# Token tiles loaded from ScalarE's queue beside weights from SyncE's, and two reordered places in a one-core hybrid block

## The chip, the cores and the metric

The kernel runs on one core of a Trainium2 chip. The metric is the device time of one execution in microseconds (us), lower is better. Five engines share the core's on-chip memory: TensorE (PE, matmuls into PSUM), VectorE (DVE), ScalarE (ACT), GpSimd (POOL) and SyncE (SP, which here does little but issue transfers). Each engine works through its own list of instructions in order; semaphores make one wait for another. A DMA is issued by an engine and then carried out by 16 DMA engines beside it.

## What is computed

One layer of a hybrid encoder block on 256 tokens of width 2048, float32. Cut to what matters:

```
u = rms_norm(x, norm_mix_pre)
proj = u @ w_in                        # q/k/v of two attentions, RWKV-7 inputs, three gates
y_a = stick_breaking_attention(...);  y_b = forgetting_attention(...);  y_c = rwkv7_time_mix(...)
m = g_a * (y_a @ w_branch_a) + g_b * (y_b @ w_branch_b) + g_c * (y_c @ w_branch_c)
x = x + rms_norm(m @ w_out, norm_mix_post)
hdn = square(relu(rms_norm(x, norm_mlp_pre) @ w_mlp_up))        # 2048 -> 8192
x = x + rms_norm(hdn @ w_mlp_down, norm_mlp_post)
```

The change touches the first lines (how `x` and the first weights come in), the step from `m @ w_out` to `w_mlp_up`, and the last line.

## The kernel before, in words

**Weights.** All weights lie in one array `wst` of pieces of 128 x 1024 floats (512 KB). They stream through three buffers `raw`. Each piece is split into a rounded high part (`whi`, an ACT copy) and the rest (`wlo`, a DVE subtraction); activations are split the same way into the two halves of a tile `pk`. A product is then high x both halves (a matmul of 512 columns) and low x high (256 columns). `wsplit` (L151) does the split; a new piece may be loaded only when the DVE has read the old one out of its buffer.

**Who decides the order.** A scheduler places the instructions on the engines; in the first part, up to `written.close()` (L1273), PE's order is the order in which the code is written. `tc.issue_after` makes an instruction come after a named one on its engine. A DMA gets one of eight completion semaphores in turn, and an issue whose semaphore still belongs to an earlier DMA waits until that one has landed, on the queue of the engine that issues it.

**Begin** (L264 to L369). The token matrix, transposed, is `X0`: 16 tiles of 128 x 256 (tile k holds features 128k to 128k+127). `loadx(a, b)` loads tiles a to b-1, `load(n, q)` half q of weight piece n, `con` and `ident` are constants. All of these are issued by SP. Three products `qb` are built at once: pieces 0, 2, 4 with tiles 0 to 7, then pieces 1, 3, 5 with tiles 8 to 15. `xsplit(k)` (L311) makes `pk` of tile k, `wpart` (L319) splits half a piece, `prods` (L328) issues the matmuls. Five matmuls on zeros (L273) run before the data come.

**Passage** (L1166 to L1272). For the second half of the tokens (`tt` = 1) the residual sum `x1[1]` is finished in strips of 256 columns (`add_mixed`, L1182, DVE) while it is already transposed and used. In the loop over k2 = 0, 2, ... 14, `turned(k2, 1)` (L1220) transposes two 128 x 128 blocks of `x1[1]` into one half of the PSUM tile `trs[k2 // 2]`; ACT and DVE read that tile into two tiles `pk` (L1254, L1260); and `both(k2 - 2)` (L1230) runs the eight matmuls of the two tiles before with two weight pieces. The blocks of the first token half are transposed by `turn_first` (L1223), which also takes a new PSUM tile. There are four such tiles (`mps`, four buffers): four `turn_first` come before the loop, and the fifth, sixth, ... need a tile that ACT and DVE have read to the end.

**End** (L1592 to L1619). The last product comes in two token halves of 128 rows. For each half, for the last strip of 512 columns: DVE adds PSUM into `y` (L1603), ACT squares with a running sum (L1604), `rstd_of` turns that into a factor `rs` (DVE L1165, POOL L1166), `gained` multiplies by the gain (L1607), and four DVE instructions of 512 columns (L1618) each followed by a store of 256 KB (L1619) give the output.

Of the kernel before, what the change touches and what calls it, by code (L numbers as in the profile page):

```python
# [12 lines left out]
AF = mybir.ActivationFunctionType  # L13
ALU = mybir.AluOpType
# [4 lines left out]
D = 2048  # L19
# [31 lines left out]
def hybrid_block(ctx, tc, xt, x, gains, params, consts, lora, gup, wst, out):  # L51
    nc = tc.nc
    V, A, G, PE = nc.vector, nc.scalar, nc.gpsimd, nc.tensor
# [11 lines left out]
    def nm(s):  # L65
        uid[0] += 1
        return f"{s}_{uid[0]}"
# [15 lines left out]
    par = cpool.tile([128, NPAR], F32, name="par")  # L83
# [7 lines left out]
    def P(name, i=0, r=slice(0, 128)):  # L91
        return par[r, PC[name] + i:PC[name] + i + 1]
# [135 lines left out]
    def pin(ins):  # L228
        return tc.keep_in_program_order(ins)
# [33 lines left out]

    dum = cpool.tile([128, 1], F32, name="dum")  # L264
    G.memset(dum, 0.0)
    A.activation(dum, dum, AF.Tanh)
    X0 = rp.tile([128, KT, T], F32, tag="SC", name="x0", bufs=1)
    A6 = rp.tile([128, 6, T], F32, tag="b6", name="a6", bufs=1)
    zt = rp.tile([128, T], F32, tag="tha", name="zt", bufs=1)
    V.memset(zt, 0.0)  # L270
    idle = mps()
    for i in range(5):
        PE.matmul(idle[:, 0:T], zt[:, 0:128], zt, start=True, stop=True)  # L273
    nc.sync.dma_start(out=par, in_=params)
    raws = {}

    def load(n, q=None):

        if n not in raws:
            raws[n] = wpool.tile([128, HALF], F32, tag="raw", name=nm("raw"), bufs=3)  # L280
        cs = slice(0, HALF) if q is None else slice(512 * q, 512 * q + 512)
        nc.sync.dma_start(out=raws[n][:, cs], in_=wst[n][:, cs])

    def loadx(a, b):
        nc.sync.dma_start(out=X0[:, a:b, :], in_=xt[:, a:b, :])

    loadx(0, 2)
    load(0, 0)
    loadx(2, 4)
    load(2, 0)  # L290
    load(4, 0)
    loadx(4, 8)
    for n in (0, 2, 4):
        load(n, 1)
    loadx(8, 12)
    side.append(lambda: nc.sync.dma_start(out=con, in_=consts[:, 128:]))
    side.append(lambda: nc.sync.dma_start(out=ident, in_=consts[:, 0:128]))
    cst = cpool.tile([128, 4], F32, name="cst")
# [12 lines left out]
    def xsplit(k):  # L311
        u = pk()
        split(X0[:, k, :], u, P("g1", k))
        upk.append(u)

    qb = [gps() for _ in range(3)]
    w = {}
# [92 lines left out]
    for h in range(8):  # L410
        ps = qb[h] if h < 3 else unit(upk)
# [641 lines left out]
    for s in ("q", "k"):  # L1053
        lst = []
        for h in range(4):
            ps = unit(upk)
# [12 lines left out]
    for hf in range(2):  # L1069
        for s, mo in (("k", MU_K), ("r", MU_R), ("v", MU_V)):  # L1070
            for p in range(4 * hf, 4 * hf + 4):
                ps = unit(upk)
# [84 lines left out]
    def rstd_of(ss, eps, sums):  # L1157

        if sums is None:
            sums = cpool.tile([128, 1], F32, name=nm("ssum"))  # L1160
            V.tensor_reduce(sums, ss[:, 0:3], AX.X, ALU.add)
            V.tensor_scalar(sums, sums, 1.0 / D, eps, ALU.mult, ALU.add)
            return sums
        r = cpool.tile([128, 1], F32, name=nm("rs"))
        V.tensor_scalar(r, ss[:, 3:4], 1.0 / D, sums, ALU.mult, ALU.add)  # L1165
        G.tensor_tensor(r, r, cst[:, 2:3], ALU.pow)  # L1166
        return r

    g2, loads = gain(0, [fm().rearrange("p a b -> p (a b)")[:, 0:512] for _ in range(4)])
    x1 = [p2.tile([128, D], F32, tag="x1", name=nm("x1"), bufs=2) for _ in range(2)]  # L1170
    for c in range(0, D, 512):
        for tt in range(2):
            loads.append(lambda tt=tt, c=c: nc.sync.dma_start(out=x1[tt][:, c:c + 512],
                                                              in_=x[tt * 128:tt * 128 + 128, c:c + 512]))
# [15 lines left out]
    for g in range(4):  # L1190
# [4 lines left out]
        for tt, ps in enumerate(tok(mpk, 5 if g == 3 else 1)):  # L1195
            def gained():
                return V.tensor_tensor(mg[tt][:, gs], ps, g2[g], ALU.mult)
# [18 lines left out]
    trs = []  # L1216
# [6 lines left out]
    def turn_first():  # L1223
        trs.append(mps())
        turned(2 * len(trs) - 2, 0)
# [23 lines left out]
    for k2 in range(0, KT, 2):  # L1249
        turned(k2, 1)  # L1250
        src = [trs[k2 // 2][:, i * T:i * T + T] for i in range(2)]
        us = [pk(), pk()]
        for i, u in enumerate(us):
            queued(0, lambda: A.activation(u[:, 0:T], src[i], AF.Copy, scale=P("g3", k2 + i)))  # L1254
        if k2 == 8:
            queued(1, pend)
        if k2 + 2 < KT:
            queued(1, lambda: add_mixed(1, 128 * k2 + 256, 256))
        for i, u in enumerate(us):
            queued(1, lambda: V.scalar_tensor_tensor(u[:, T:], src[i], P("g3", k2 + i), u[:, 0:T].bitcast(F32),  # L1260
                                                     ALU.mult, ALU.subtract))
        upk2.extend(us)
        if k2:
            both(k2 - 2)
        if len(trs) < 8:
            turn_first()
        if k2 in (2, 6, 10):
            with tc.issue_after(chain[0].ins), tc.issue_after(chain[1].ins):
                wsplit(wraw(base + {2: 1, 6: 3, 10: 4}[k2]))
            if k2 < 10:  # L1270
                whl.append(wq.pop(0))
# [65 lines left out]
    eps4, sum4 = [], []  # L1337
    ss4 = cpool.tile([128, 2, 4], F32, name="ss4")
    ys = []
# [177 lines left out]
    for j in range(2):  # L1517
        up(j)
        ps, post = heads[j]
# [72 lines left out]
    for g in range(4):  # L1592
        gs = slice(512 * g, 512 * g + 512)
        if g == 2:
            assert not threads
            spare.clear()
            x1 = [p2.tile([128, D], F32, tag="x1", name=nm("x1"), bufs=2) for _ in range(2)]
            for tt in range(2):
                for c in (0, 1024):
                    nc.sync.dma_start(out=x1[tt][:, c:c + 1024], in_=xs[tt][:, c:c + 1024])  # L1600
        for tt, ps in enumerate(tok(hp, 3 if g == 3 else 1)):
            yv = ys[tt][:, gs]
            V.tensor_tensor(yv, yv, ps, ALU.add)  # L1603
            A.activation(junk(), yv, AF.Square, accum_out=ss4[:, tt, g:g + 1])  # L1604

            def gained():
                V.tensor_tensor(yv, yv, g4[g], ALU.mult)  # L1607

            if g < 3:
                gained()  # L1610
                if g == 2:
                    sum4.append(rstd_of(ss4[:, tt, :], eps4[tt], None))
            else:
                r4 = rstd_of(ss4[:, tt, :], None, sum4[tt])
                gained()
                for c in range(0, D, 512):
                    cs = slice(c, c + 512)
                    V.scalar_tensor_tensor(x1[tt][:, cs], ys[tt][:, cs], r4, x1[tt][:, cs], ALU.mult, ALU.add)  # L1618
                    nc.sync.dma_start(out=out[tt * 128:tt * 128 + 128, cs], in_=x1[tt][:, cs])  # L1619


# [123 lines left out]
```

## Time and profile before

| What | Value |
|---|---|
| Time, three runs | 1502.9, 1503.46 (median), 1503.58 us |
| Profiled execution | 1500.87 us, span 1499.1 us |
| Mean granted TensorE clock | 0.997 |
| Busy: DVE | 1215.9 us (81%) |
| Busy: ACT | 934.6 us (62%) |
| HBM read / written | 282.65 MB / 4.19 MB |

The span runs from the first to the last instruction of the profiled execution; the execution's own time is 1.77 us longer. In the views below, times are us from the start of the span. A row of the timeline gives start, length, engine, line, operation, the tile written and those read, how many instructions were merged, and in brackets how long the engine had been idle before it and what ended that. "SPq" is SP issuing a DMA.

### The profile page before, as it was taken

Reading aid. Unit: us, or ns where it says so; the run is one execution under the profiler, and the core shown is the slowest. Engines: PE = TensorE matmul, PEld = TensorE weight load, DVE = VectorE, ACT = ScalarE, POOL = GpSimd, SP = SyncE. Lnnn points to the kernel's source line nnn. Section 1 sums busy time; section 2 is a strip of 40 time slices with the busy share of each in tenths; the row PEclk is TensorE's granted clock in tenths of the full one; section 3 lists DMA queues with packets and bytes.
Section 4 is the critical chain, followed back from the end, with each engine's and each line's share of the span. In section 5 each row is a group of like instructions: output and inputs, shape, how many; then the busy total and the mean of one; then the engine's idle time right before and its main releaser. Section 6 shows DMA issues by size and latency. Waiting matters only on the chain.

```text
span 1499.1 us, 22798 instructions
## 1 busy us (share of the span) xinstructions
PE 1479.3 (99%) x8401; PEld 1248.4 (83%) x8401; DVE 1215.9 (81%) x1687; ACT 934.6 (62%) x1396; POOL 91.2 (6%) x160
## 2 busy tenths in 40 slices
PE   9999999999999999999998999999999999999997
PEld 7888888888778888788887888888888888888885
DVE  7576678899679798567646788999899989899986
ACT  7565666664576554474444766777767766767662
POOL 0021000100001100000000000000000000000000
PEclk9999999999999999999999999999999999999999
DMA  7545545445544546445755868888888888889874
GB/s 267 191 152 188 170 169 183 168 162 195 172 156 168 177 166 209 143 159 189 275 191 181 278 216 250 253 253 264 240 257 246 269 252 233 254 241 266 279 244 152
DMA packets 107615, 317.70 MB, mean 212 GB/s; under 512 B 10736, under 2 KB 14704, under 8 KB 107248
## 3 DMA queue, kind: packets, MB, share of 16 engines
q1 hardware_dynamic: 94832, 284.91, 55.1%
q0 software_dynamic: 8064, 29.36, 10.5%
q10 hardware_dynamic: 4608, 1.97, 0.5%
q8 instruction: 66, 1.08, 0.3%
q14 instruction: 45, 0.37, 0.1%
HBM read 282.65 MB, written 4.19 MB: 191 GB/s over the span
## 4 chain that ended last, share of the span: by engine, by line
PE 94%; DVE 2%; DMA 1%; ACT 1%; issue 1%; POOL 0%; SPq 0%; POOLq 0%; DVEq 0%; ACTq 0%
PE gps L220 28%; PE gps L174 22%; PE gps L178 12%; PE gps L204 7%; PE mps L1469 3%; PE mps L1470 3%; PE mps L1471 3%; PE gps L1471 2%; PE gps L1469 2%; PE gps L1470 2%; PE gps L182 1%; DMA x<-in_xt_dram 1%; DMA raw<-in_wst_dram 1%; PE mps L789 1%; DVE wlo L159 1%
## 5 line engine op out<-in xcount | busy, mean ns | idle before, releaser
L159 DVE TENSOR_TENSOR wlo<-raw,whi 128x1024 fp32r<-128x1024 f32 x497 | 602.7, 1221 | 152.1 <-ACT whi L158 136.8
L158 ACT ACTIVATE whi<-raw 128x1024 fp32r<-128x1024 f32 x497 | 523.0, 1057 | 247.9 <-PE gps L220 85.4
L174 PE MATMUL gps<-pk,whi 128*128 128x512 f32 x1336 | 336.5, 391 | 0.4 <-ACT whi L158 0.4
L174 PEld LDWEIGHTS gps<-pk,whi 128*128 128x128 f32 x1336 | 247.3, 188 | 48.8 <-ACT whi L158 0.6
L220 PE MATMUL gps<-whi,pk 128*128 128x512 f32 x1136 | 286.0, 391 | 0.0
L220 PEld LDWEIGHTS gps<-whi,pk 128*128 128x128 f32 x1136 | 211.5, 188 | 44.0
L178 PEld LDWEIGHTS gps<-pk,wlo 128*128 128x128 f32 x1424 | 194.1, 190 | 14.1 <-DVE wlo L159 0.3
L178 PE MATMUL gps<-pk,wlo 128*128 128x256 f32 x1424 | 199.3, 282 | 0.0
L220 PE MATMUL gps<-wlo,pk 128*128 128x512 f32 x568 | 155.2, 392 | 0.0
L220 PEld LDWEIGHTS gps<-wlo,pk 128*128 128x128 f32 x568 | 105.6, 188 | 21.9
L1332 DVE TENSOR_TENSOR sp<-raw,sp 128x1024 fp32r<-128x1024 f32 x67 | 81.8, 1220 | 3.3 <-ACT sp L1331 3.1
L1360 ACT ACTIVATE sp<-gps 128x512 f32<-128x512 f32 x52 | 31.0, 597 | 83.0 <-PE gps L182 83.0
L1331 ACT ACTIVATE sp<-raw 128x1024 fp32r<-128x1024 f32 x67 | 70.7, 1055 | 14.3 <-PE mps L1470 4.7
L204 PE MATMUL gps<-whi,pk 128*128 128x512 f32 x256 | 68.9, 390 | 0.0
L1469 PE MATMUL mps<-whi,fm 128*128 128x512 f32 x168 | 66.1, 394 | 0.0
L1470 PE MATMUL mps<-whi,fm 128*128 128x512 f32 x168 | 65.8, 392 | 0.0
L1471 PE MATMUL mps<-wlo,fm 128*128 128x512 f32 x168 | 65.5, 390 | 0.0
L1431 POOL DMA_DIRECT2D raw<-raw x40 | 34.9, 874 | 431.6 <-DVE wlo L159 106.7
L204 PEld LDWEIGHTS gps<-whi,pk 128*128 128x128 f32 x256 | 47.8, 188 | 9.9
L1471 PE MATMUL gps<-wlo,fm 128*128 128x512 f32 x126 | 49.3, 391 | 0.4 <-DVE wlo L159 0.4
L1469 PE MATMUL gps<-whi,fm 128*128 128x512 f32 x126 | 49.2, 391 | 0.0
L1428 DVE TENSOR_TENSOR raw<-raw,raw 128x1024 f32<-128x1024 f32 x40 | 48.8, 1221 | 0.4
(390 smaller groups left out, 2006.0 us busy)
## 6 DMA issues: line engine op xcount, KB each, us to landing
raw<-in_wst_dram SPq DMA_DIRECT2D x499, 512.0 KB, 4.3
raw<-raw POOLq DMA_DIRECT2D x40, 512.0 KB, 6.6
sp<-in_wst_dram SPq DMA_DIRECT2D x16, 512.0 KB, 5.5
raw<-sp POOLq DMA_DIRECT2D x8, 512.0 KB, 6.7
sp<-raw POOLq DMA_DIRECT2D x8, 512.0 KB, 6.9
x<-in_x_dram SPq DMA_DIRECT2D x8, 256.0 KB, 5.5
xs<-x SPq DMA_DIRECT2D x2, 1024.0 KB, 4.3
x<-xs SPq DMA_DIRECT2D x4, 512.0 KB, 5.9
```

Of the source, the lines that this page charges most:

```text
L158: A.activation(hi, raw, AF.Copy)
L159: V.tensor_tensor(lo, raw, hi.bitcast(F32), ALU.subtract)
L174: PE.matmul(ps, hi[:, i * 128:i * 128 + 128], pks[i], start=first and i == 0, stop=False)
L178: PE.matmul(ps[:, 0:T], lo[:, i * 128:i * 128 + 128], pks[i][:, 0:T], start=False, stop=False)
L204: PE.matmul(ps[tt], pks[k][:, c:c + 128], w[:, (k - k0) * 512:(k - k0) * 512 + 512], start=k == 0 and part == 0 and w is hl[0], stop=w is ...
L220: PE.matmul(ps[tt], pks[k][:, c:c + 128], w[:, (k - k0) * 512:(k - k0) * 512 + 512], start=k == 0 and part == 0 and w is hl[0], stop=False)
L1331: A.activation(hi, raw, AF.Copy)
L1332: V.tensor_tensor(lo, raw, hi.bitcast(F32), ALU.subtract)
L1428: V.tensor_tensor(x, x, z, ALU.add)
L1469: PE.matmul(Q[f], p, w, start=d == 0 and i == 0, stop=False)
L1470: PE.matmul(Q[f], pl, w, start=False, stop=False)
L1471: PE.matmul(Q[f], p, wl, start=False, stop=d == nd - 1 and i == 1)
```

## The change

Three edits.

1. Begin: the loads of token tiles 0 to 11 move from SP's queue to ACT's: two loads of two tiles each, then the small activation `warm` (which loads ACT's function table), then two loads of four tiles each. SP issues the parameters, the six weight halves, and then what follows; tiles 12 to 15 stay on SP.
2. Passage: `turn_first` inside the loop is moved under `if k2:`, so that it is not called at k2 = 0.
3. End: of the four last DVE instructions of token half 0, two stay where they were and two come after the DVE addition of half 1 (`added`). For half 1 the last strip of 512 columns is done as two of 256.

```diff
-    A.activation(dum, dum, AF.Tanh)
     X0 = rp.tile([128, KT, T], F32, tag="SC", name="x0", bufs=1)
+    def loadx(a, b, queue=nc.sync):
+        return queue.dma_start(out=X0[:, a:b, :], in_=xt[:, a:b, :])
+    nc.sync.dma_start(out=par, in_=params)
+    for a in (0, 2):
+        first_x = loadx(a, a + 2, nc.scalar)
+    with tc.issue_after(first_x.ins):
+        warm = A.activation(dum, dum, AF.Tanh)
+    with tc.issue_after(warm.ins):
+        for a in (4, 8):
+            last_x = loadx(a, a + 4, nc.scalar)
...
-    loadx(0, 2)
-    load(0, 0)
-    loadx(2, 4)
-    load(2, 0)
-    load(4, 0)
-    loadx(4, 8)
-    for n in (0, 2, 4):
-        load(n, 1)
-    loadx(8, 12)
+    for q in range(2):
+        for n in (0, 2, 4):
+            load(n, q)
...
         if k2:
             both(k2 - 2)
-        if len(trs) < 8:
-            turn_first()
+            if len(trs) < 8:
+                turn_first()
...
-            V.tensor_tensor(yv, yv, ps, ALU.add)
+            added = V.tensor_tensor(yv, yv, ps, ALU.add)
...
-            else:
-                r4 = rstd_of(ss4[:, tt, :], None, sum4[tt])
+                continue
+            def final(c, w):
+                cs = slice(c, c + w)
+                V.scalar_tensor_tensor(x1[tt][:, cs], ys[tt][:, cs], r4, x1[tt][:, cs], ALU.mult, ALU.add)
+                nc.sync.dma_start(out=out[tt * 128:tt * 128 + 128, cs], in_=x1[tt][:, cs])
+            if tt == 0:
+                r4 = rstd_of(ss4[:, 0, :], None, sum4[0])
                 gained()
-                for c in range(0, D, 512):
+                final(0, 512)
+                final(512, 512)
+                r40 = r4
+                continue
+            with tc.issue_after(added.ins):
+                for c in (1024, 1536):
                     cs = slice(c, c + 512)
-                    V.scalar_tensor_tensor(x1[tt][:, cs], ys[tt][:, cs], r4, x1[tt][:, cs], ALU.mult, ALU.add)
-                    nc.sync.dma_start(out=out[tt * 128:tt * 128 + 128, cs], in_=x1[tt][:, cs])
+                    V.scalar_tensor_tensor(x1[0][:, cs], ys[0][:, cs], r40, x1[0][:, cs], ALU.mult, ALU.add)
+                    nc.sync.dma_start(out=out[0:128, cs], in_=x1[0][:, cs])
+            r4 = rstd_of(ss4[:, 1, :], None, sum4[1])
+            gained()
+            for c, w in ((0, 512), (512, 512), (1024, 512), (1536, 256), (1792, 256)):
+                final(c, w)
```

The change adds lines, so a line number of the kernel after is up to 17 higher than that of the same statement before.

SP's list at the begin from the last weight half on, before (`x` is the token matrix X0, `raw` a weight piece or its half):

```order
L282 DMA raw_103<-in_wst_dram 128x512
L285 DMA x_86<-in_xt_dram 128x1024
L282 DMA raw_213<-in_wst_dram 128x1024
L285 DMA x_86<-in_xt_dram 128x1024
L282 DMA raw_216<-in_wst_dram 128x1024
L282 DMA raw_218<-in_wst_dram 128x1024
L145 DMA raw_312<-in_wst_dram 128x1024
```

and now:

```order
L292 DMA raw_105<-in_wst_dram 128x512
L269 DMA x_85<-in_xt_dram 128x1024
L297 DMA con<-in_consts_dram 128x1152
L298 DMA ident<-in_consts_dram 128x128
L292 DMA raw_213<-in_wst_dram 128x1024
L292 DMA raw_216<-in_wst_dram 128x1024
L292 DMA raw_218<-in_wst_dram 128x1024
L145 DMA raw_312<-in_wst_dram 128x1024
```

Four token loads are gone from SP. Tiles 12 to 15 stood behind `raw_213` (piece 1) and now stand ahead of it, and so do the two constants, which the scheduler had placed behind pieces 6 and 7.

ACT's list at the begin now (before, it began with the table load):

```order
L269 DMA x_85<-in_xt_dram 128x512 x2
L275 ACT_TABLE_LOAD
L275 ACTIVATE dum<-dum 128x1
L269 DMA x_85<-in_xt_dram 128x1024 x2
L242 ACTIVATE pk_123<-x_85,par 128x256
```

All four issues stand ahead of ACT's first work; the last of them has the semaphore of the first weight half and waits until that has landed.

PE's list in the passage, before (`x_1337` and `x_1338` are the two token halves of `x1`, `mps` are the tiles `trs`):

```order
L1220 MATMUL mps_7982<-ident,x_1338_7310 128x128 x2
L1220 MATMUL mps_8004<-ident,x_1337_7309 128x128 x2
L1220 MATMUL mps_7985<-ident,x_1338_7310 128x128 x2
L1235 MATMUL gps_7980<-pk_7997,whi_7918 128x512
L1235 MATMUL gps_7981<-pk_7997,w_1464_7940 128x512
L1235 MATMUL gps_7980<-pk_7998,whi_7918 128x512
L1235 MATMUL gps_7981<-pk_7998,w_1464_7940 128x512
L1239 MATMUL gps_7980<-pk_7997,wlo_7919 128x256
L1239 MATMUL gps_7981<-pk_7997,w_1465_7941 128x256
L1239 MATMUL gps_7980<-pk_7998,wlo_7919 128x256
L1239 MATMUL gps_7981<-pk_7998,w_1465_7941 128x256
L1220 MATMUL mps_8024<-ident,x_1337_7309 128x128 x2
```

and now:

```order
L1221 MATMUL mps_7982<-ident,x_1338_7310 128x128 x2
L1221 MATMUL mps_7985<-ident,x_1338_7310 128x128 x2
L1236 MATMUL gps_7980<-pk_7997,whi_7918 128x512
L1236 MATMUL gps_7981<-pk_7997,w_1464_7940 128x512
L1236 MATMUL gps_7980<-pk_7998,whi_7918 128x512
L1236 MATMUL gps_7981<-pk_7998,w_1464_7940 128x512
L1240 MATMUL gps_7980<-pk_7997,wlo_7919 128x256
L1240 MATMUL gps_7981<-pk_7997,w_1465_7941 128x256
L1240 MATMUL gps_7980<-pk_7998,wlo_7919 128x256
L1240 MATMUL gps_7981<-pk_7998,w_1465_7941 128x256
L1221 MATMUL mps_8021<-ident,x_1337_7309 128x128 x2
L1221 MATMUL mps_7988<-ident,x_1338_7310 128x128 x2
```

The first row of each is `turned(0, 1)`. The fifth `turn_first` (`mps_8004`, now `mps_8021`) has moved behind the first `both` (the eight rows of L1235 and L1239, now L1236 and L1240), and every later one moves back by one `both` as well. On DVE one pair changes places in the passage: the weight subtraction of k2 = 2 now stands ahead of the strip of `add_mixed` that it followed.

DVE's list at the end, before (`rs` are the factors of the two halves):

```order
L1618 SCALAR_TENSOR_TENSOR x_2583_14109<-y_8767,rs_14256,x_2583_14109 128x512 x4
L1603 TENSOR_TENSOR y_8768<-y_8768,gps_14204 128x512
L1165 TENSOR_SCALAR rs_14289<-ss_8164,ssum_14200 128x1
L1607 TENSOR_TENSOR y_8768<-y_8768,pk_13934 128x512
L1618 SCALAR_TENSOR_TENSOR x_2584_14110<-y_8768,rs_14289,x_2584_14110 128x512 x4
```

and now:

```order
L1618 SCALAR_TENSOR_TENSOR x_2583_14109<-y_8767,rs_14256,x_2583_14109 128x512 x2
L1604 TENSOR_TENSOR y_8768<-y_8768,gps_14204 128x512
L1631 SCALAR_TENSOR_TENSOR x_2583_14109<-y_8767,rs_14256,x_2583_14109 128x512 x2
L1166 TENSOR_SCALAR rs_14289<-ss_8164,ssum_14200 128x1
L1608 TENSOR_TENSOR y_8768<-y_8768,pk_13934 128x512
L1618 SCALAR_TENSOR_TENSOR x_2584_14110<-y_8768,rs_14289,x_2584_14110 128x512 x3
L1618 SCALAR_TENSOR_TENSOR x_2584_14110<-y_8768,rs_14289,x_2584_14110 128x256 x2
```

The addition of half 1 stands two instructions earlier, the factor of half 1 where it stood, and there is one final instruction and one store more.

More of the change, by code (lines that the diff above doesn't have):

```diff
@@ L273, in hybrid_block @@
         PE.matmul(idle[:, 0:T], zt[:, 0:128], zt, start=True, stop=True)
-    nc.sync.dma_start(out=par, in_=params)
     raws = {}
@@ L282, in load @@
         nc.sync.dma_start(out=raws[n][:, cs], in_=wst[n][:, cs])
-    def loadx(a, b):
-        nc.sync.dma_start(out=X0[:, a:b, :], in_=xt[:, a:b, :])
-    loadx(0, 2)
-    load(0, 0)
-    loadx(2, 4)
-    load(2, 0)
-    load(4, 0)
-    loadx(4, 8)
-    for n in (0, 2, 4):
-        load(n, 1)
-    loadx(8, 12)
+    for q in range(2):
+        for n in (0, 2, 4):
+            load(n, q)
     side.append(lambda: nc.sync.dma_start(out=con, in_=consts[:, 128:]))
```

## The prediction

> **What bounds the kernel now.** The page's chain of work that ended last comes first, then the view of waits for PE:
>
> ```profile
> PE 94%; DVE 2%; DMA 1%; ACT 1%; issue 1%; POOL 0%; SPq 0%; POOLq 0%; DVEq 0%; ACTq 0%
> ```
>
> ```profile
> PE mps L1220 <- DVE pk L1260: 3.0, 3, 1.9
> PE gps L334 <- DVE pk L243: 1.5, 2, 1.3
> ```
>
> The whole program is one long stretch of PE work. PE's named waits are few, and the longest ones lie in just the places that the change edits: L334 is the begin, L1220 the passage. Elsewhere PE always has work, so what is won or lost at these places moves everything behind it by as much. The third place is the tail after PE's last matmul, where DVE, POOL and the stores follow each other. So I price three stages apart and add.
>
> **Begin.** The timeline, then the chain in order of time, the windows, and two transfers, each from a stretch that holds its issue alone (KB, us to landing):
>
> ```profile
> 4.21 0.91 ACT L242 ACTIVATE pk<-x,par 128x256 fp32r<-128x256 f32 x2 [1.98 <-DMA x<-in_xt_dram]
> 5.02 0.61 ACT L325 ACTIVATE whi<-raw 128x512 fp32r<-128x512 f32 x1
> 7.13 0.91 ACT L242 ACTIVATE pk<-x,par 128x256 fp32r<-128x256 f32 x2 [1.49 <-DMA x<-in_xt_dram]
> 12.07 0.33 SPq L282 DMA_DIRECT2D raw<-in_wst_dram  x1
> 13.07 1.70 ACT L242 ACTIVATE pk<-x,par 128x256 fp32r<-128x256 f32 x4
> 17.86 1.70 PE L334 MATMUL gps<-pk,whi 128*128 128x512 f32 x4 [0.25 <-DVE pk L243]
> ```
>
> ```profile
> 19.55 0.96 PE gps L332 x8
> 20.51 1.84 PE gps L334 x8
> ```
>
> ```profile
> 0.00:7.00 7.00, 5.73 (x12) 3.70 (x12) 2.28 (x7) 2.91 (x5) 2.18 (x15) 1.00 0.59 183
> 7.00:12.00 5.00, 3.79 (x21) 3.18 (x22) 3.74 (x8) 4.26 (x9) 0.00 (x0) 1.00 0.96 375
> 12.00:13.00 1.00, 1.00 (x8) 0.71 (x7) 1.00 (x4) 1.00 (x3) 0.00 (x0) 1.00 0.12 49
> ```
>
> ```profile
> raw<-in_wst_dram SPq DMA_DIRECT2D x1, 512.0 KB, 3.2
> x<-in_xt_dram SPq DMA_DIRECT2D x1, 512.0 KB, 6.8
> ```
>
> The last three numbers of a windows row are the granted clock, the busy share of the DMA engines and GB/s. Until 12 us ACT waits for data again and again; then SP has nothing to issue, because the next buffer is free only at 12.07, and the DMA engines stand nearly idle for 1 us. Piece 1 lands 3.2 us after its issue, at 15.27, and tiles 12 to 15, issued behind it, hold PE: its first matmuls on them at 17.86 run at DVE's pace, 1.70 us for four where eight take 1.84. From there PE runs through, and the group of piece 1 ends at 19.55 + 0.96 = 20.51.
>
> Now tiles 12 to 15 come before piece 1, so PE's group of piece 1 hangs on piece 1 alone. If that lands at L, ACT copies half of it (0.61), and PE needs 1.84 + 0.96: the group ends at L + 3.4. It breaks even at L = 17.1; the begin is worth 17.1 - L.
>
> L by bytes: ahead of piece 1 now stand the parameters (58 KB), all of x (2048), six halves of 256, `con` (576) and `ident` (64), with piece 1 itself 4794 KB, or 4.91 MB. By 12 us the trace had moved 7 x 183 + 5 x 375 = 3156, or 3.16 MB. The other 1.75 MB at 375 GB/s take 4.7 us, to 16.7. A landing comes later than the bytes' turn: piece 1, with little ahead of it, took 3.2 where its 512 KB at 375 GB/s take 1.4, and of the 1.8 between I count 0.8 as behind the last byte. Since two engines issue side by side, data start about one issue earlier, 0.4 (0.33 in the row of 12.07, and a gap). That is **L = 17.1, begin 0.0 us**. So what x's last tiles gain, the constants ahead of piece 1 use up; PE did not need them that early.
>
> Bounds: piece 1 is of no use before ACT has made the seven tiles that stand ahead of it, from 13.07 at 1.70 / 4 each, 16.0, which gives +1.1. At worst piece 1 takes as long as the slowest load here, 6.8 from 12.07: L = 18.9, -1.8. The four issues on ACT cost it some 0.4 us each ahead of its first copy, and the last waits for the first weight half (there by the copy of 5.02 before), so the first copy moves from 4.21 to 5.3 or more. This is covered: ACT waits for tiles 2 and 3 till 7.13 anyway. If that cover went, at most the 1.49 us of that row would be lost. The five matmuls on zeros, the table load and the parameters do not move on the path.
>
> The Trainium skill, "DMA: Bandwidth & Descriptors", section Issuing engines are not separate DMA queues, says that queues of several engines run on the same 16 DMA engines and that a second one saves only issue time; it speaks against this edit. By that rule the begin is worth no more than the 0.0 above, and a rate better than 183 GB/s in the first 7 us is not to be had.
>
> **Passage.** Timeline, chain and windows:
>
> ```profile
> 810.33 0.44 PE L1220 MATMUL mps<-ident,x 128*128 128x128 f32 x2 [1.30 <-DVE x L1182]
> 810.81 0.84 ACT L1254 ACTIVATE pk<-mps,par 128x256 fp32r<-128x256 f32 x2 [1.92 <-PE mps L1220]
> 811.68 0.88 DVE L1260 SCALAR_TENSOR_TENSOR pk<-mps,par,pk 128x256 fp32r<-128x256 f32 x2 [1.01 <-ACT pk L1254]
> 812.47 0.48 DVE L1182 SCALAR_TENSOR_TENSOR x<-mg,rs,x 128x256 f32<-128x256 f32 x1
> 812.70 1.01 PE L1220 MATMUL mps<-ident,x 128*128 128x128 f32 x4 [1.93 <-DVE pk L1260]
> 821.01 0.68 DVE L1197 TENSOR_TENSOR mg<-gps,fm 128x512 f32<-128x512 f32 x1
> 821.61 1.22 DVE L159 TENSOR_TENSOR w<-raw,w 128x1024 fp32r<-128x1024 f32 x1
> ```
>
> ```profile
> 813.71 1.71 PE gps L1235 x4
> 815.42 0.85 PE gps L1239 x4
> ...
> 825.57 0.93 PE gps L1235 x4
> 826.50 0.47 PE gps L1239 x4
> 826.96 0.22 PE mps L1220 x2
> 827.18 1.83 PE gps L174 x8
> ...
> 831.32 0.47 PE gps L1239 x4
> ```
>
> ```profile
> 813.00:814.00 1.00, 1.00 (x6) 0.90 (x5) 0.00 (x0) 0.25 (x1) 0.00 (x0) 0.50 0.00 0
> 809.00:812.30 3.30, 0.47 (x3) 0.20 (x2) 1.64 (x5) 0.84 (x2) 0.54 (x1) 1.00 0.85 308
> ```
>
> Before, each round is one chain: the fifth `turn_first` waits for DVE's read of the first tile and holds up `turned(2, 1)`, which does not need it; every later round repeats this with the next tile, about 2.6 us (transposes 0.6, ACT 0.84, DVE 0.88, gaps), while eight matmuls take 0.93 + 0.47 = 1.40. The last `both` ends at 831.8.
>
> After, I walk the new lists with the lengths of these rows, in us:
> - `turned(2, 1)` follows `turned(0, 1)` at once, and ACT's second pair its first, to 812.4. DVE has the first `pk` at 812.2; its strip (0.48) and second pair end at 813.7.
> - PE: first `both` 812.25 to 813.65, two times two transposes (0.22 each), second `both` from 814.1 to 815.5, then 0.44 and 1.40 in turn: 815.9 to 817.3, 817.8 to 819.2.
> - Here DVE is late: the gain (0.68) and a weight subtraction (1.22) stand ahead of the next strip, which is done at 820.05. `turned(10, 1)` at 820.1, `both` 820.6 to 822.0 and 822.2 to 823.6, transposes, eight L174 (1.83) to 825.6, two last `both` to **828.4**.
>
> The same walk over the old lists ends at 831.9, as the trace does within 0.1, so the steps are the right ones. That makes 3.4 us. But the profiled execution had a slow stretch: the granted clock was 0.50 at 813 to 814, and the first `both` took 1.71 + 0.85 = 2.56. With 1.40 there, the walk over the old lists ends at 830.75, and the gain is 2.3. With such a stretch after the change too it is 1.6 (end at 830.2). The three timed runs do not show their clocks. I take the new kernel at full clock, since its longest stretch without products, from 809.0 to 812.25, is 3.2 us where the old one's was over 4 (to the products after the transposes of 812.70), and the middle between 2.3 and 3.4 for the old runs: **passage +2.8 us**, ends 0.5 (old at full clock, new slow) and 3.4. The DVE pair that changes places costs nothing: PE is in its second `both` when the later strip is done, at 815.25.
>
> The Trainium skill, "TensorE: Matmul & The Clock Gate", Part 1, has a free-running window of about 3.4 us, after one idle of which the clock is halved. The trace agrees with the half clock; by the rule a stretch of 3.2 us never holds an idle window, and the passage would be worth 2.3 or 3.4, never 1.6.
>
> **End.** Timeline, and the last store:
>
> ```profile
> 1487.07 2.74 DVE L1618 SCALAR_TENSOR_TENSOR x<-y,rs,x 128x512 f32<-128x512 f32 x4 [0.46 <-POOL rs L1166]
> 1487.68 0.61 PE L204 MATMUL gps<-wlo,fm 128*128 128x512 f32 x2
> 1489.72 0.68 DVE L1603 TENSOR_TENSOR y<-y,gps 128x512 f32<-128x512 f32 x1
> 1491.25 0.21 DVE L1165 TENSOR_SCALAR rs<-ss,ssum 128x1 f32<-128x1 f32 x1 [0.85 <-ACT junk L1604]
> 1492.51 2.74 DVE L1618 SCALAR_TENSOR_TENSOR x<-y,rs,x 128x512 f32<-128x512 f32 x4 [0.44 <-POOL rs L1166]
> ```
>
> ```profile
> out_dram<-x SPq DMA_DIRECT2D x1, 256.0 KB, 2.8
> ```
>
> PE is done at 1488.29, but the addition waits behind four instructions of 0.66 us each (1487.07 to 1489.72, by four). After two it starts at 1488.40, 1.3 us sooner. Then two final instructions of half 0 run while ACT squares: 0.60 (0.68 less an overlap of 0.08) + 2 x 0.66 put `rs` at 1490.33, not 1.53 after the addition but 1.93; it is 0.9 sooner. 1.26 later (as 1491.25 to 1492.51) come three strips of 0.66 and two of 256 columns (0.40 and 0.48, the pair of 811.68): end 1494.47 against 1492.51 + 2.74 = 1495.25. The last store still lands some 2.8 later. **End +0.8**; 0.5 if the smaller store lands as slowly behind its neighbour, 1.0 if it is quicker by its size.
>
> **Sum.** 0.0 + 2.8 + 0.8 = 3.6 us. Against the profiled execution's own 1500.87 the terms are 0.0 + 3.4 + 0.8 = 4.2, giving 1496.7; against the median of the runs, 1503.46, which lies 2.6 higher, **1499.9**.
>
> **Rivals.**
> - *The slow clock stays in the passage.* 3.2 us with four transposes is not far from what halved the clock before (0.47 us busy in 3.3). For it: nobody sees the threshold; against it: 0.67 us of transposes and products from 812.25. Then 0.0 + 1.6 + 0.8 = 2.4: 1501.1. Chance 0.25.
> - *The begin loses.* ACT's queue takes half the rate while SP's weights and the constants stand in line; piece 1 at 18.9: -1.8 + 2.8 + 0.8 = 1.8, 1501.7. Chance 0.15.
> - *The begin wins.* The 183 GB/s of the first 7 us were one queue's limit, and two fill the engines: +1.1 + 2.8 + 0.8 = 4.7, 1498.8. Chance 0.12.
> - *Slower than before.* Only piece 1 can do it: each us past 17.1 is a us of PE idle, so the gains of 3.6 are gone at L = 20.7, 8.6 us after its issue. No load of the begin took over 6.8. At L = 23.7 it would be 1506.5. Chance 0.03.
>
> The forecast has 0.45. A difference of 0.2% (3.0 us) is about what a measurement of this kernel can tell from no change. Faster by more needs a time under 1500.5: most of the forecast (0.36), the begin that wins (0.12) and some of the first rival (0.06): 0.54. Slower by more: 0.02. The rest, 0.44, within. Range: from 1.1 + 3.4 + 0.9 = 5.4 less, to the passage at 1.6, the end at 0.6 and half the loss at the begin, 0.9, together 1.3 less: 1498.1 to 1502.2.
>
> **What would show it.** Begin: piece 1 lands near 17, L334's group of it ends near 20.5, no wait for x after 13 us. Passage: no wait of PE for `pk` L1260 of more than 0.5 us except before the first product, one for the strip at k2 = 10; the first `both` in 1.4 us; the last `both` some 19.4 us after PE's last W_out product, not 22.8. End: the addition of half 1 within 0.2 us of PE's last matmul, the last DVE instruction 6.2 us after it, not 7.0. It is wrong if the weights of the MLP come too late for the earlier PE (a new wait on DMA after 828), or if the begin's first copies slip past 7 us.

## The result and the profile after

| | before | after |
|---|---|---|
| time, median of 10 runs each (us) | 1502.05 | 1499.32 |
| ratio to before, 95% interval | | 0.9980 (0.9971 to 0.9988) |
| profiled execution: time, span (us) | 1500.87, 1499.1 | 1497.57, 1495.7 |

The changed kernel is 0.2% faster: 3.0 us by the ratio, 1.8 to 4.4 by its interval. The forecast was 3.6 and 1499.9. One of before's ten executions took 2467.78 us and does not enter the ratio; without it before's median is 1501.74.

PE's named waits after the change, in us in total, times, longest:

```profile
PE mps L1221 <- DVE x L1183: 1.8, 2, 1.3
PE gps L335 <- DVE pk L243: 1.6, 1, 1.6
PE gps L1236 <- DVE pk L1261: 1.0, 1, 1.0
```

The three waits for `pk` ahead of transposes (3.0 us before) are gone. What is left in the passage is the first wait for the strip (1.3), the one ahead of the first product (1.0), and one of 0.5. At the begin the two waits for `pk` (1.3 at 8.21, behind the first two products, and 0.25 at 17.86) have become one of 1.6, ahead of the first product.

**Begin.** Timeline of the changed kernel, rows of the three engines that matter, and its chain in order of time:

```profile
5.47 0.33 ACTq L269 DMA_DIRECT2D x<-in_xt_dram  x1
5.92 0.91 ACT L242 ACTIVATE pk<-x,par 128x256 fp32r<-128x256 f32 x2 [2.77 <-DMA raw<-in_wst_dram]
7.39 3.70 PE L335 MATMUL gps<-pk,whi 128*128 128x512 f32 x8 [1.58 <-DVE pk L243]
...
13.27 2.00 PE L335 MATMUL gps<-pk,whi 128*128 128x512 f32 x8
...
17.07 1.15 ACT L326 ACTIVATE whi<-raw 128x512 fp32r<-128x512 f32 x2 [0.71 <-DMA raw<-in_wst_dram]
18.13 0.49 ACT L242 ACTIVATE pk<-x,par 128x256 fp32r<-128x256 f32 x1
...
19.48 0.19 PEld L335 LDWEIGHTS gps<-pk,whi 128*128 128x128 f32 x1 [0.25 <-DVE pk L243]
```

```profile
12.53 4.45 DMA raw<-in_wst_dram
17.75 2.23 PE gps L335 x8
19.98 0.95 PE gps L333 x8
```

ACT's fourth issue (5.47) stands ahead of its first copy (5.92), and what ended ACT's wait is a weight's landing. PE's first product comes at 7.39 (before 5.69), and its first eight take 3.70 us where eight take 2.00 later: PE works at half pace here. Piece 1, issued at 12.53, lands at 16.98. The last of x's tiles is copied only behind piece 1 (18.13), and the last of the eight products waits 0.25 us for it (19.48; PEld is PE loading its weights). The group ends at 19.98 + 0.95 = 20.93, where it was 20.51.

**Passage.** The chain of the changed kernel, then windows (span of the window; busy us of PE, PEld, DVE, ACT, POOL; granted clock, DMA share, GB/s); the first windows row is of the begin:

```profile
812.65 2.07 PE gps L1236 x4
814.73 0.85 PE gps L1240 x4
...
821.69 0.41 DVE x L1183
822.10 0.04 issue
822.14 0.44 PE mps L1221 x2
...
830.24 0.47 PE gps L1240 x4
```

```profile
0.00:7.00 7.00, 4.63 (x10) 3.19 (x10) 1.25 (x6) 2.57 (x5) 2.18 (x15) 1.00 0.68 220
...
809.26:812.67 3.41, 1.07 (x7) 0.42 (x5) 1.65 (x5) 1.49 (x5) 0.54 (x1) 1.00 0.98 333
812.67:816.08 3.41, 3.41 (x12) 3.02 (x13) 3.03 (x6) 1.09 (x2) 0.00 (x0) 0.50 0.03 11
```

The slow stretch of the kernel before is here again, of the same length, behind a window in which PE was busy for 1.07 of 3.41 us. The first `both` takes 2.07 + 0.85 = 2.92 us instead of 1.40.

**End.** Timeline of the changed kernel:

```profile
1485.00 0.61 PE L204 MATMUL gps<-wlo,fm 128*128 128x512 f32 x2
1485.71 0.68 DVE L1604 TENSOR_TENSOR y<-y,gps 128x512 f32<-128x512 f32 x1
...
1488.88 2.87 DVE L1618 SCALAR_TENSOR_TENSOR x<-y,rs,x 128x512 f32<-128x512 f32 x5 [0.44 <-POOL rs L1167]
```

The addition of half 1 starts 0.1 us after PE's last matmul (1485.61), and DVE is done 6.1 us after it (1491.75), where it was 6.9.

**A stretch nobody touched.** From the passage's last product to PE's last matmul it took 1488.29 - 831.79 = 656.5 us before and 1485.61 - 830.71 = 654.9 after. Of this, 1.1 us are two waits in PE's list of before that the list after has not:

```profile
PE gps L1471 <- DVE sp L1332: 0.7, 1, 0.7
PE gps L1471 <- DVE wlo L159: 0.4, 1, 0.4
```

So the 3.3 us between the two spans (1499.06 and 1495.75) are not the sum that was forecast. They are -0.4 (begin), +1.5 (passage), +0.6 (end) and +1.6 of this stretch.

### The profile page after: what moved, and what is told of

Read it like the earlier page. It is cut to its first block, busy times and chain, and to the rows that moved or that the text cites. A ratio compares the mean times of both kernels' runs of the same rounds, so it can differ in the third digit from the quotient of the medians.

```text
span 1495.7 us, 22805 instructions
## 1 busy us (share of the span) xinstructions
PE 1479.1 (99%) x8401; PEld 1249.2 (84%) x8401; DVE 1215.3 (81%) x1688; ACT 934.2 (62%) x1396; POOL 91.1 (6%) x160
## 4 chain that ended last, share of the span: by engine, by line
PE 96%; DVE 1%; ACT 1%; DMA 1%; issue 1%; POOL 0%; SPq 0%; POOLq 0%; DVEq 0%; ACTq 0%
PE gps L220 28%; PE gps L174 23%; PE gps L178 13%; PE gps L204 7%; PE mps L1470 3%; PE mps L1471 3%; PE mps L1472 3%; PE gps L1472 3%; PE gps L1470 3%; PE gps L1471 3%; PE gps L182 2%; DMA raw<-in_wst_dram 1%; PE mps L790 1%; PE gps L1236 0%; PE gps L335 0%
```

## The experiments

The theory is that each edit is worth what its own stage shows, that the passage's gain depends on whether the clock is halved there, and that the 1.6 us behind it are luck. The rivals are that the clock is mostly full, that the change itself shortens the stretch behind the passage, and that the begin is worth nothing or wins.

One table for all, worked out from each run's trace. First product: start of PE's first product of the begin. Group: end of the low products of piece 1. Passage: from the start of its first transposes to its last product (the first four expectations count from the end of W_out's last product, which makes it 0.2 shorter). Behind: from there to PE's last matmul. Last DVE: end of the last DVE instruction after that. Half clock gives the stretches with a granted clock of 0.50. In some profiles the records of the granted clock begin only behind the first product. "Pace" means that until then the products' length alone tells the half clock: 0.63 us and more for one of 512 columns, where it is 0.39 later (the windows show a clock of 1.00 there).

| run | ratio to before (95%) | first product | half clock at the begin | group | passage | half clock there | behind | last DVE |
|---|---|---|---|---|---|---|---|---|
| before | | 5.69 | pace, to 7.3 | 20.51 | 23.8 | 812.8 to 816.2 | 656.5 | 6.9 |
| before_again | 1.0000 (0.9991 to 1.0009) | 6.18 | pace, to 7.1 | 21.05 | 23.5 | 812.6 to 816.0 | 658.4 | 6.9 |
| after | 0.9980 (0.9971 to 0.9988) | 7.39 | pace, to 10.5 | 20.93 | 22.3 | 812.7 to 816.1 | 654.9 | 6.1 |
| after_again | 0.9986 (0.9977 to 0.9995) | 8.11 | 7.6 to 14.4 | 22.57 | 20.7 | none | 656.3 | 6.1 |
| begin_only | 0.9995 (0.9986 to 1.0004) | 7.31 | 9.3 to 12.7 | 21.14 | 23.0 | none | 656.0 | 6.9 |
| passage_only | 0.9978 (0.9969 to 0.9987) | 5.97 | pace, to 6.5 | 20.77 | 20.7 | none | 659.2 | 6.9 |
| end_only | 0.9990 (0.9981 to 0.9999) | 6.16 | 7.7 to 14.5 | 22.17 | 22.9 | none | 657.0 | 6.1 |
| no_begin | 0.9976 (0.9967 to 0.9985) | 6.83 | 8.3 to 11.7 | 21.25 | 22.2 | 813.9 to 817.3 | 658.5 | 6.1 |
| warm | 0.9976 (0.9968 to 0.9984) | 7.21 | 8.4 to 11.8 | 20.89 | 20.7 | none | 654.8 | 6.1 |
| late_gain | 0.9976 (0.9968 to 0.9985) | 7.86 | pace, to 13.9 | 22.20 | 20.3 | none | 659.3 | 6.1 |
| late_constants | 0.9982 (0.9973 to 0.9990) | 7.97 | 8.8 to 12.2 | 21.49 | 20.7 | none | 658.8 | 6.1 |
| warm_begin | 0.9977 (0.9967 to 0.9987) | 5.96 | pace, to 6.8 | 21.04 | 20.3 | none | 659.1 | 6.1 |
| two_on_act | 0.9966 (0.9952 to 0.9979) | 5.89 | none | 19.40 | 23.5 | 810.5 to 817.3 | 658.4 | 6.1 |
| combined | 0.9963 (0.9951 to 0.9976) | 6.04 | none | 19.68 | 20.3 | none | 657.3 | 6.1 |

The ratios are over 5 to 12 runs of each kernel; the profile shows one of them.

### Each part alone

`begin_only` has only this part of the change:

```diff
+    for a in (0, 2):
+        first_x = loadx(a, a + 2, nc.scalar)
...
+    with tc.issue_after(warm.ins):
+        for a in (4, 8):
+            last_x = loadx(a, a + 4, nc.scalar)
...
+    for q in range(2):
+        for n in (0, 2, 4):
+            load(n, q)
```

> Only the begin is edited, passage and end stay as before. Theory (each edit is worth what its own stage shows in the profile of the changed kernel): piece 1 lands near 17.0, tile 15's copy on ACT stands behind piece 1's, the first low products of piece 1 end near 20.9 (before 20.51), so W_out's last product ends near 808.6 (before 808.18): 0.4 us lost, 1.0003 of before. Rival (the begin is worth 0.0 as predicted, the 0.4 was one execution): 20.5 and 808.2. Rival (two queues win): under 19.5. Passage 23.6 us and end 7.0 as before. The 654.9 us from the last product of the passage to PE's last (656.5 before) stay at 656.5 if they hang on the passage.

The group ended at 21.14, 0.6 behind the profile of before, and the passage at full clock took 23.0 us instead of 23.8. So before's slow stretch is not in every execution of the old code. The ratio holds 1.

`passage_only`:

```diff
         if k2:
             both(k2 - 2)
-        if len(trs) < 8:
-            turn_first()
+            if len(trs) < 8:
+                turn_first()
```

> Only the passage is edited. Theory: from W_out's last product to the passage's last product 22.1 us (before 23.6), with the half clock for 3.4 us from about 812.3: 1.5 us gained, 0.9990. Rival (the clock stays full here in most executions): 20.2 us and 3.4 gained, 0.9977. Second question, the stretch from the passage's last product to PE's last: 656.5 if the 1.6 us that it lost in the changed kernel's profile were the luck of the loads in that execution, 654.9 if the passage's edit causes it; then 0.9979.

Windows of its profile, in the passage's gap:

```profile
808.59:812.00 3.41, 2.06 (x14) 1.29 (x12) 1.34 (x4) 1.10 (x4) 0.54 (x1) 1.00 0.99 336
812.00:815.42 3.42, 2.42 (x15) 2.11 (x16) 2.96 (x6) 2.40 (x6) 0.00 (x0) 1.00 0.31 125
```

Here the clock stays full and the passage takes 20.7 us, as the rival has it, while the stretch behind it took 659.2: 2.7 more than before, and neither of the values asked about. So the half clock comes and goes with the execution, and the length of what lies behind does too.

`end_only` and `no_begin` (passage and end of the change, with the begin of before):

```diff
+            with tc.issue_after(added.ins):
+                for c in (1024, 1536):
...
+            for c, w in ((0, 512), (512, 512), (1024, 512), (1536, 256), (1792, 256)):
+                final(c, w)
```

> Only the end is edited. Theory: from PE's last matmul to the last DVE instruction 6.1 us (before 7.0), 0.8 gained, 0.9995, the rest as before: passage 23.6, the stretch behind it 656.5. Rival (that stretch varies from execution to execution): it lies anywhere from 654.9 to 656.5 or more, and the time with it.

> The change without its begin. Theory: 0.4 us faster than the whole change: W_out's last product at 808.2, passage 22.1, end 6.1; 2.3 us gained by these stages, 0.9985, and 0.9974 if the 1.6 us behind the passage belong to the change. Rival (the begin is worth nothing): as the whole change, 0.998.

The end is 6.1 in every kernel that has the edit and 6.9 in every other (6.14 and 6.95 before rounding, a difference of 0.8). Between the last DVE instruction and the end of the span there are 3.8 us without it and 3.9 to 4.0 with it, so some 0.2 of the 0.8 go to the last store. Windows of `no_begin`:

```profile
810.47:813.88 3.41, 1.28 (x6) 0.70 (x6) 1.87 (x5) 1.86 (x5) 0.50 (x1) 1.00 0.82 308
813.88:817.29 3.41, 3.41 (x14) 3.12 (x13) 2.59 (x5) 1.06 (x3) 0.00 (x0) 0.50 0.05 11
```

With the same passage as `passage_only`, a window that happens to cover the gap has PE busy for 1.28 us and is followed by half clock; the two windows above split the gap, with 2.06 and 2.42. The windows lie differently to the program in each execution.

### Is it the clock?

`warm` is the whole change with PE kept busy in the gap. The extra matmuls write a buffer that the first `both` starts afresh:

```diff
+    def fill():
+        for _ in range(2):
+            PE.matmul(pair[1][:, 0:T], C("ident"), x1[0][:, 0:T], start=True, stop=True)
+
     for _ in range(4):
         turn_first()
+    fill()
...
+        if k2 == 2:
+            fill()
         if k2:
             both(k2 - 2)
```

> The whole change, and four extra matmuls on data that nobody reads in the two gaps of the passage in which PE waits (two after the first transposes, two ahead of the first product), so that PE is busy for over 2.5 us of any 3.41 us there. Theory (the clock is halved when PE was busy for less than some 1.4 us of a stretch of 3.41 us whose start falls differently in each execution: 0.53, 1.07 and 1.29 us were followed by half, 1.48 to 2.36 by full): never halved here, 20.7 us from the end of W_out's products to the passage's last product (the whole change had 22.3, the passage alone at full clock 20.7); time 0.4 to 1.0 us under the whole change, about 0.9975 of before. Rival (the half clock comes from the products' start itself, not from the idle gap): a row at 0.5 again, 22.3. Rival (the extra matmuls delay the transposes): later than 20.7 at full clock, with a first product after 813.2.

Window and chain of its profile:

```profile
810.48:813.90 3.42, 2.95 (x14) 2.06 (x15) 2.42 (x7) 2.52 (x5) 0.00 (x0) 1.00 0.64 248
```

```profile
812.65 1.19 PE gps L1236 x4
813.84 0.48 PE gps L1240 x4
...
828.66 0.47 PE gps L1240 x4
```

The first product starts at 812.65, as in the profile of the change, and with the same start the passage ends at 829.13 instead of 830.71. So the clock is worth 1.6 us here and the extra matmuls cost nothing. All four kernels that have them (`late_gain`, `warm_begin` and `combined` below too) had full clock in the passage; in the two windows that hold the gap PE was never busy for less than 2.79 us there. Full clock was granted in three of the six changed passages without them, so four of four alone would be luck one time in sixteen; the busy time is what sets the four apart. The gain over the whole change is too small for the ratios to tell (0.9976 beside 0.9980 and 0.9986).

`late_gain` is `warm` with DVE's read of W_out's sum moved behind the strip:

```diff
-        if k2 == 8:
-            queued(1, pend)
         if k2 + 2 < KT:
             queued(1, lambda: add_mixed(1, 128 * k2 + 256, 256))
...
+        if k2 == 8:
+            queued(1, pend)
         upk2.extend(us)
```

> As the kernel with the extra matmuls, and the gain of the last half (DVE's read of W_out's sum) is put behind the strip and the splits at k2 = 8 instead of ahead of them. Theory (the 0.5 us for which PE waits for the strip is DVE's queue: gain 0.68 and weight 1.22 ahead of it): that wait goes, the passage takes 20.2 us. Rival (the wait moves to the split of k2 = 8, which now stands behind the weight subtraction): a wait of 0.5 us or more for that split, passage 20.7 or more.

PE's waits in its passage:

```profile
PE mps L1221 <- DVE x L1183: 0.4, 1, 0.4
PE gps L1236 <- DVE pk L1264: 0.2, 1, 0.2
```

The wait for the strip at k2 = 10 is gone (0.4 is the first one). A wait on splits of 0.2 is listed, as in `warm` already; the passage is 20.27 us, 0.43 less, and 20.3 in the two other kernels with this edit.

### What the begin hides

`late_constants`, the change with the constants behind piece 5:

```diff
+    def constants(dst, src):
+        with tc.issue_after(piece3.ins):
+            nc.sync.dma_start(out=dst, in_=src)
...
     for n in (3, 5):
-        load(n)
+        piece3 = load(n)
```

> The whole change, with the two loads of constants (640 KB) issued behind pieces 1, 3 and 5, where the kernel before had them behind piece 1 too. Theory (the constants ahead of piece 1 use up what x's last tiles gain): piece 1 lands 1.7 us sooner (640 KB at 375 GB/s), near 15.3; ACT's seven tile copies then bound it (16.4), and the low products of piece 1 end near 20.2 where the whole change had 20.93. Rival (the landing hangs on the issue, which waits for a buffer till 12.5, and on what x still moves): lands near 17 as before, 20.9.

Timeline of its profile:

```profile
15.66 1.14 ACT L330 ACTIVATE whi<-raw 128x512 fp32r<-128x512 f32 x2
...
18.54 2.00 PE L339 MATMUL gps<-pk,whi 128*128 128x512 f32 x8
```

ACT copies piece 1 at 15.66 without a wait, so it had landed by then: 3.6 us at most behind its issue at 12.06, where the whole change took 4.45 from 12.53. So the constants hold piece 1 back, but by less than was expected: in the three kernels that have them behind it (this one, `two_on_act` and `combined`) it landed at 15.4, 15.6 and 15.9, in the five executions with the begin of the change at 15.9 to 17.0, which is 0.7 us later in the mean and not 1.7. And the group ended at 21.49. From 9.09 on PE had no wait of note, part of that at half clock, and reached piece 1 only at 18.54. The bound was not the landing but PE's late start and its clock.

`warm_begin` has the begin of before with two extra matmuls on zeros, and `late_gain`'s passage and the end:

```diff
         prods(0, ks[0:2], False)
+        if q == 0:
+            for _ in range(2):
+                PE.matmul(idle[:, 0:T], zt[:, 0:128], zt, start=True, stop=True)
```

> The begin as before the change, with two extra matmuls on zeros behind the first two products; passage as in the kernel with the gain moved; end as in the change. Theory (the half clock at the begin too comes from a stretch of 3.41 us in which PE is nearly idle; it was half for one or two such stretches in three of six executions, whose low products of piece 1 ended at 21.1 to 22.2 where the three others had 20.5 to 20.9): full clock from its first row to 20 us, the low products of piece 1 end at 20.5 to 20.8; passage 20.2, end 6.2; 4 us under before, 0.997. Rival (the begin's spread comes from the landings, not from the clock): full clock, but 21 or later. Rival (extra matmuls stand in the way of the third product): it starts after 8.8.

Timeline of its profile:

```profile
16.00 1.15 ACT L325 ACTIVATE whi<-raw 128x512 fp32r<-128x512 f32 x2 [1.21 <-DMA raw<-in_wst_dram]
...
17.18 1.71 ACT L242 ACTIVATE pk<-x,par 128x256 fp32r<-128x256 f32 x4
```

ACT waits 1.21 for piece 1 and has the last four tiles from 17.18 on only. The clock was full, yet the group ended at 21.04: with the old begin the landings set the end, as that rival has it.

### The same kernels again, and two better ones

`before_again` and `after_again` are the two kernels unchanged.

> The kernel before, unchanged, for a second profile. Theory (the 1.6 us between the passage's end and PE's last matmul are no part of the change: in eleven executions of old and new kernels so far it was 654.8 to 659.3 us long): it lies in that range and not again at 656.5; passage 23.0 at full clock or 23.8 with the half clock; end 7.0; ratio 1.000. Rival (every stage repeats for one kernel): 656.5 and 23.8 again.

> The changed kernel, unchanged, for a second profile. Theory: end 6.2; passage 20.7 at full clock or 22.3 with the half clock, after a stretch of 3.41 us with PE busy for less than 1.4; ACT's first copy of the begin at 5.9 or later; the stretch behind the passage anywhere in 654.8 to 659.3. Rival (the change shortens that stretch): 654.9 again.

Behind the passage before_again took 658.4 and after_again 656.3. Over all executions this stretch is 656.0 to 658.4 with the old passage (four, mean 657.0) and 654.8 to 659.3 with the new one (ten, mean 657.7). The 1.6 us of the profiled pair are luck. The begin of `after_again`, windows:

```profile
4.18:7.59 3.41, 0.89 (x4) 0.44 (x3) 0.42 (x2) 0.96 (x3) 0.00 (x0) 1.00 0.99 358
7.59:14.42 6.83, 6.31 (x16) 4.81 (x17) 6.80 (x15) 6.83 (x16) 0.00 (x0) 0.50 1.04 406
```

PE waits for its first product and is busy for 0.89 of 3.41 us; then it has half clock for two such stretches. Its first eight products:

```profile
8.11 4.05 PE L335 MATMUL gps<-pk,whi 128*128 128x512 f32 x8 [3.04 <-DVE pk L243]
```

From 8.11 to the end of the group PE then has no wait of 0.06 us or more.

`two_on_act` takes the last two of ACT's loads off its queue:

```diff
-    with tc.issue_after(warm.ins):
-        for a in (4, 8):
-            last_x = loadx(a, a + 4, nc.scalar)
...
     for q in range(2):
         for n in (0, 2, 4):
             load(n, q)
+        loadx(4 + 4 * q, 8 + 4 * q)
```

> The whole change, but only the first two loads of x stay on ACT's queue, the others go to SP's, between the halves of the weights. Theory (the last of ACT's four issues waits for another load's landing and so holds ACT's first copy back to 5.9 and PE's first product to 7.4; PE's idleness there then costs half clock at 7 to 14 us): first copy by 4.5, first product by 6.0; full clock from 7 or 8 us on; the low products of piece 1 end at 20.5 or earlier (20.9 to 22.2 in five executions of the new begin). Rival (x's landings hold the first copy anyway): first copy after 5, and 20.9 or later.

Timeline of its begin, and its clock in the passage:

```profile
3.88 0.91 ACT L242 ACTIVATE pk<-x,par 128x256 fp32r<-128x256 f32 x2 [0.71 <-DMA x<-in_xt_dram]
...
5.89 0.73 PE L333 MATMUL gps<-pk,whi 128*128 128x512 f32 x2 [0.45 <-ACT whi L324]
```

```profile
807.07:810.49 3.42, 1.70 (x12) 1.02 (x10) 1.09 (x3) 1.47 (x5) 0.54 (x1) 1.00 1.01 327
810.49:817.31 6.82, 6.19 (x21) 5.43 (x22) 4.85 (x10) 2.57 (x6) 0.00 (x0) 0.50 0.45 174
```

The first copy is at 3.88, the first product at 5.89, the clock full, and the group ends at 19.40: earlier than in any of the ten executions of the old or the changed begin (20.51 to 22.57). In this build the scheduler also put the constants behind pieces 1, 3 and 5 and tile 15 ahead of piece 1, so the run shows the three together. Its passage had bad luck: half clock for two stretches, 23.5 us.

`combined` has `two_on_act`'s loads, the late constants, the extra matmuls and the later gain of the passage, and the end.

> Two loads of x on ACT's queue and the rest on SP's, constants behind pieces 1, 3 and 5, the passage with the four extra matmuls and the later gain, the end of the change. Theory: the low products of piece 1 end near 20.2, passage 20.3, end 6.2: 0.6 + 3.0 + 0.7 = 4.3 us under before, 0.9971. Rival (the spread behind the passage hides what stands ahead of it): those three stages, but no ratio under 0.9975.

Group 19.68, passage 20.3, end 6.1. Its ratio, 0.9963 (0.9951 to 0.9976), is the lowest, 5.6 us under before. It lies below that of the change, and the ends of the two intervals overlap by little. The sum of its stages against the means of the old ones (21.15 and 23.3, below) is 1.5 + 3.0 + 0.6, some 5.1; the interval is too wide to tell its gain over `two_on_act` alone.

## Why the prediction was right, and where it was not

The time, the sign and the range came out; of the steps below the sum, two did not.

**Begin, forecast 0.0.** In the profile of the change the landing was as forecast, L = 17.1 and 16.98 measured. That is partly luck: in the four other executions of the changed begin piece 1 landed at 15.9 to 16.3, and with the mean of all five, 16.3, the forecast's own sum would have given +0.8. The group was to end at L + 3.4. In this profile it ended 0.55 later, of which 0.25 is the wait for the tile whose copy stood behind piece 1's on ACT (19.48). In the four others PE had no wait of 0.06 us or more at piece 1, so its landing did not set the end there: PE's late start and its clock did. The step that failed is "This is covered: ACT waits for tiles 2 and 3 till 7.13 anyway". The first copy did slip, to 5.92 (5.3 or more was forecast), but the cover is one of ACT's data. PE's first product slipped with it, from 5.69 to 7.39, and PE's idleness there costs clock: in all five executions of the changed begin the first product was at 7.2 or later and PE ran at half clock or half pace for 3.1 us or more behind it. In the old begin it did so in two of five, and in the three others for 1.2 us or less, with no more than two products. Group ends: old 20.51, 21.05, 20.77, 22.17, 21.25, mean 21.15; changed 20.93, 22.57, 21.14, 20.89, 22.20, mean 21.55. That is -0.4 us, within the bounds given, and less than the spread of one kernel; the ratios (0.9995 for the begin alone, 0.9976 without it beside 0.9980 and 0.9986 with it) do not tell it from nothing. ACT's issue, held by a landing, is what keeps the copy back: in all six executions with four loads on ACT the fourth starts 0.02 us after the first weight half has landed (5.47 behind 5.45 after the change), and in `two_on_act`, without it, copy and product come 2.0 and 1.5 us sooner than after the change.

The Trainium skill ("DMA: Bandwidth & Descriptors", Issuing engines are not separate DMA queues) was read as: no better rate than 183 GB/s in the first 7 us. The rate was better, 220 in the row above; how much of that is saved issue time was not separated. PE gained nothing by it, as the forecast had it.

**Passage, forecast +2.8, the term that was mis-sized.** Both ends were right: at full clock the passage went from 23.0 to 20.7, 2.3 us as walked; with half clock on both sides from 23.8 and 23.5 to 22.2 and 22.3, 1.4 for the walked 1.6. The new kernel with the slow stretch was walked to 830.2, and ended at 830.71 with the begin 0.4 later. What failed is the choice between them: "I take the new kernel at full clock, since its longest stretch without products, from 809.0 to 812.25, is 3.2 us", with the rival at 0.25; three of the six changed passages read had the slow stretch. It is not products that count but how busy PE is in a window that lies anywhere, and the gap is covered by one window in some executions and split in others. Nor does the slow stretch cost the old passage the 1.15 us of the walk (831.9 against 830.75): 23.5 and 23.8 with it, 22.9 and 23.0 without. The old passage was halved in two of four executions (mean 23.3), the changed one in two of five (22.3, 20.7, 20.7, 22.2, and 20.7 of `late_constants`; mean 21.3): 2.0 us. With `two_on_act`, which had two halved stretches, three of six, and 1.6 us.

The Trainium skill ("TensorE: Matmul & The Clock Gate", Part 1) was taken to exclude the halving, because no window of 3.4 us was idle. The length agrees (3.41 us), but the window need not be idle: 1.07 us busy was enough.

**End, forecast +0.8.** 6.9 to 6.1 in DVE's part in every run, less some 0.2 for the last store: 0.6, inside 0.5 to 1.0.

**Sum.** -0.4 + 2.0 + 0.6 = 2.2 us by stages, beside the 3.0 (1.8 to 4.4) and 2.1 (0.8 to 3.5) of the two comparisons; 3.6 was forecast. The agreement of 1499.9 with 1499.32 is partly luck with the base: before had a median of 1503.46 over the three runs known then, 1501.74 over the nine of the result that enter the ratio, and 1502.3 to 1502.43 in the later comparisons. The gain was forecast too large by 0.6 to 1.5, the base too high by 1.0 to 1.7. No new wait of the MLP on DMA came from the earlier PE as far as the ten executions tell: their stretch is 0.7 longer in the mean, with a spread of 4.5.

What stays open: what decides between 654.8 and 659.3 behind the passage. PE's waits of over 0.12 us there add up to nothing in the two shortest and to 2.5 in the longest; those listed are for weights. The other 2.0 of the 4.5 us stand in no wait of PE. No run took that apart.

## What to carry to other kernels

A load issued from a computing engine can hold that engine until another load has landed: count what stands behind the issue on that engine, and give it only those issues that do not have to wait. Where PE waits for a few us, ask what its clock will be afterwards; harmless matmuls in the gap settle it. Price a stage from several executions: here the stages of one kernel differ by 1 to 4 us, more than the whole change.

## What the runs showed of the chip that was not expected

- The halved clock comes in stretches of 3.41 us (or two, 6.83), whose start falls differently in each execution. Ahead of one that followed full clock, PE was busy for 0.89, 1.07, 1.28, 1.59 (`end_only`, begin) and 1.70 us of the 3.41 (`two_on_act`, passage), among others; in `begin_only` a window from 811.45 with 1.53 was followed by full clock, and so was every one read with 1.78 or more. So the limit lies near 1.6 of 3.41 in these runs, and busy time alone does not draw it sharply.
- Such a stretch costs about 1.6 us in the changed passage (22.2 and 22.3 beside 20.7), 0.5 to 0.9 in the old one, and can recur: at 7.6 to 14.4 PE was busy for 6.31 of 6.83 us at half clock. At half clock, 2.65, 2.78 and 2.89 busy us of 3.41 were followed by another such stretch, 2.78 once and 3.1 or more always by full clock.
- The first 7 us moved 180 to 194 GB/s in the six executions with one queue and 220 to 243 in the eight with two.
- A stretch of 655 us that no edit touched took 654.8 to 659.3 us from execution to execution.
